# Gate accumulation pinned to its place in the vector queue, and a split moved behind two products

## The chip, the cores and the metric

The kernel runs on one core of one Trainium2 chip. The metric is device microseconds of one execution; the median of several runs counts. Within the core, TensorE (PE) multiplies, VectorE (DVE), ScalarE (ACT) and GpSimd (POOL) work element by element, and SyncE (SP) issues most of the loads. Each engine takes its instructions from its own queue, in order.

## What is computed

Two layers of a diffusion backbone, for 128 context tokens and 512 latent tokens (640 in all, width 1024). Layer 0 mixes tokens with attention and a state-space scan, layer 1 with pooling. Each layer ends with a dense SwiGLU feed-forward network (FFN). The change lies in the FFN and in the gates that scale its output:

```python
def modulation(cvec, w_mod, b_mod):
    m = jnp.expand_dims(jax.nn.silu(cvec) @ w_mod + b_mod, -2)
    return split_last(m, (D_MODEL,) * 6)          # shift, scale, gate of both sub-layers

def swiglu(h, w_gate, w_up, w_down):
    return (jax.nn.silu(h @ w_gate) * (h @ w_up)) @ w_down
...
fp = swiglu(modulate(xp, norm_pre_ffn[l], shf_p, scf_p), ffn_w_gate[l], ffn_w_up[l], ffn_w_down[l])
xp = xp + gf_p * rmsnorm(fp, norm_post_ffn[l])    # gf: gate, from the modulation
```

Everything is float32. A product is made of three matmuls over a high and a low part of each operand (high by high, high by low, low by high), so each weight and each activation is first split into two parts.

## The kernel before

**The FFN** (`_ffn`, line 538) has 22 tiles of 128 hidden columns, taken in 11 pairs. Each pair has two matrices, gate and up. The first pair is done by `plain` (line 644) in eight products. The other 20 matrices run in one loop (line 686, `n` from 2 to 21; even `n` is gate, odd is up), each by seven block products p1, p2, p5, p6, p7, p4, p3 of 12 matmuls over 320 columns (line 535). Between the products, five calls of `d()` (line 699) each do one piece of the down projection of the pair before (`down_add`, line 626: six matmuls of lines 98 to 100, then an add into `y` at line 632; for the first pair a ScalarE copy, line 630), and then one step of background work, `net.bg()` (line 149). The last pair's matrices (n=20, 21) have no down pieces, but call the background work.

**The path from a product to the next.** p1 fills PSUM bank A, and line 569 on ScalarE copies it out. p6 adds to the same bank, so it waits for line 569. Likewise line 579 copies p6's result before p7, and line 587 copies p7's before p4. p3 ends the matrix: line 596 (VectorE) adds, then line 598 (ScalarE, gate) or line 600 (VectorE, up). Line 574 (VectorE) adds p2's result, line 588 p7's. `out_split` (line 606) splits a finished ff tile into `ah` (ScalarE, line 609) and `al` (line 610, GpSimd or VectorE); the down pieces need both. The weights are split by `split` (lines 90 and 91: `ha`, `la` and so on; `hw`, `lw` are those of the down projection). GpSimd makes the sums of weight blocks (`adds`, lines 505 to 508). `A.fourth()` (line 432) splits the block `s4` of the activations into `a2h` and `a2l` (lines 441, 442).

**The gates.** `mod_gate_mac` (line 279) computes one half (512 columns) of one gate on VectorE as background work. It is a generator; each `yield` ends a step. For each of four `u` it loads 512 KB into `mraw` (line 289, SyncE; one buffer), and two steps later and again one step later makes a pair of multiply-adds into `macc` (line 295, 128x512). The first pair reads the bias `bb`. Then for both vectors `v` a ScalarE copy (line 303) and a VectorE subtract (line 304) split the sum, two matmuls (308, 309) add up the partitions, line 310 scales, and line 311 stores to `gd` in DRAM. Two steps lie between the split and the matmuls. That is 22 steps per half, 16 of them for the accumulation. Layer 0 queues four halves (88 steps), layer 1 two (44). They are queued by `env["gates"]()` at n=4 (line 690).

**What sets the order.** The kernel is written as one sequence. A planner fixes the order of each engine's queue when the program is built: it goes through the written instructions with its own estimate of times, and puts an instruction on its engine as soon as its inputs are ready by that estimate, earlier-written ones first where several are ready. So an instruction can stand in its queue ahead of others that were written before it. At run time the queues are fixed, and each instruction waits for what it needs.

Of the kernel before, what the change touches and what calls it, by code (L numbers as in the profile page):

```python
# [9 lines left out]
F32 = mybir.dt.float32  # L10
F32R = mybir.dt.float32r
BF16 = mybir.dt.bfloat16
AF = mybir.ActivationFunctionType
ALU = mybir.AluOpType
# [31 lines left out]
class Net:  # L46
# [144 lines left out]
    def mod_pairs(self, q, load, bufs):  # L191
# [13 lines left out]
                yield None  # L205
        yield out

    def mod_vec_tile(self):
        return self.md.tile([P, KC, 2], F32, tag="mv", name=self.name("mv"), bufs=6)

# [68 lines left out]
    def mod_gate_mac(self, dst, l, j, half, gain):  # L279
        nc = self.nc  # L280
        c0 = half * 512
        bb = self.bb
        gb = self.mrp.tile([P, 512], F32, tag="gb", name=self.name("gb"), bufs=1)
        nc.scalar.dma_start(bb[0:1], self.t["b_mod"][l, j * D + c0 : j * D + c0 + 512].unsqueeze(0))
        nc.scalar.dma_start(gb, self.t[gain][l, c0 : c0 + 512].partition_broadcast(P))
        acc = self.mrp.tile([P, 2, 512], F32, tag="macc", name=self.name("macc"), bufs=1)
        for u in range(4):
            x = self.mrp.tile([P, 1024], F32, tag="mraw", name=self.name("mraw"), bufs=1)
            nc.sync.dma_start(x, self.t["w_mod"][l, 2 * j + half, u])
            yield  # L290
            yield
            for k2 in range(2):
                kc = 2 * u + k2
                for v in range(2):
                    nc.vector.scalar_tensor_tensor(  # L295
                        acc[:, v], x[:, k2 * 512 : k2 * 512 + 512], self.silc[:, kc, v : v + 1],
                        acc[:, v] if kc else bb, op0=ALU.mult, op1=ALU.add,
                    )
                yield
        for v in range(2):  # L300
            h = self.mrp.tile([P, 512], F32R, tag="modh", name=self.name("modh"), bufs=1)
            lo = self.mrp.tile([P, 512], F32R, tag="modl", name=self.name("modl"), bufs=1)
            nc.scalar.activation(h, acc[:, v], AF.Copy)
            nc.vector.tensor_tensor(lo, acc[:, v], h.bitcast(F32), ALU.subtract)
            yield
            yield
            out = self.pt([P, 512])
            nc.tensor.matmul(out, self.oner, h, start=True, stop=False)
            nc.tensor.matmul(out, self.oner, lo, start=False, stop=True)
            nc.vector.tensor_tensor(acc[:, v], out, gb, ALU.mult)  # L310
            nc.scalar.dma_start(dst[v : v + 1, c0 : c0 + 512], acc[0:1, v])
            yield
# [225 lines left out]
def _ffn(net, l, A, fr, sp, tails, switch, finish):  # L538
    nc, t = net.nc, net.t
# [66 lines left out]
    def out_split(g, f, eng=None):  # L606
        ah = env["at"].tile([P, TOK], F32R, tag="ah", name=net.name("ah"))
        al = env["at"].tile([P, TOK], F32R, tag="al", name=net.name("al"))
        nc.scalar.activation(ah, g.s[:, f], AF.Copy)  # L609
        (eng or nc.gpsimd).tensor_tensor(al, g.s[:, f], ah.bitcast(F32), ALU.subtract)  # L610
        return ah, al

    def down_load(q, dh):
        return net.raw(t["w_down"][l, q, dh])
# [11 lines left out]
    def down_add(tt, dh, parts, first):  # L626
        out = down(tt, dh, parts)
        yd = env["y"][:, tt, dh * 512 : dh * 512 + 512]
        if first:
            nc.scalar.activation(yd, out, AF.Copy)  # L630
        else:
            nc.vector.tensor_tensor(yd, yd, out, ALU.add)  # L632
# [9 lines left out]
    s0 = sp.tile([P, 2, TOK], F32, tag="sg", name=net.name("sg"))  # L642

    def plain(m, f, half):
        out = net.pt([P, HB])
        wh, wl = (x.rearrange("p (k n) -> p k n", k=KC) for x in w0[m, f])
        net.mm3(out, [(wh[:, k], wl[:, k], bh, bl) for k, (bh, bl) in enumerate(A.plain(half))])
        d = s0[:, f, half * HB : half * HB + HB]
        if m is g0:
            nc.scalar.activation(d, out, AF.Silu)  # L650
        else:
            nc.vector.tensor_tensor(d, d, out, ALU.mult)
# [23 lines left out]
    at0 = [out_split(Out(s0), 0)]  # L676
# [2 lines left out]
    plain(g0, 1, 1)  # L679
    n1.c()  # L680
    plain(u0, 1, 1)
    at0.append(out_split(Out(s0), 1, nc.vector))
    prev = at0
    wdn = net.split(fr, "w", down_load(0, 0), None)
    last = {}
    for n, m in enumerate(seq, 2):
        p, up = divmod(n, 2)
        if n == 4:
            env["gates"]()
        w = Work(m, wg if up else None)  # L690
        if not up:
            wg = w
        nx = seq[n - 1] if n - 1 < len(seq) else None
        final = p == NPAIR - 1
        if final and not up:
            last[0, 0] = net.split(fr, "w", down_load(NPAIR - 2, 0), None)
        fill = [] if final else list(range(NT))

        def d():
            if fill:  # L700
                down_add(fill.pop(0), up, [(prev, wdn)], p == 1)
            net.bg()

        if nx:
            nx.load()
        w.p1()
        w.p2()
        m.b()
        if final and up:
            last[1, 0] = net.split(fr, "a", down_load(NPAIR - 1, 0), None)  # L710
        w.p5()
        w.p6()
        m.d()
        if nx:
            nx.a()
        d()
        if n == 2:
            A.fourth()
        d()
        w.p7()  # L720
        if nx:
            nx.adds()
        d()
        if nx:
            nx.c()
        if final and up:
            last[0, 1] = net.split(fr, "c", down_load(NPAIR - 2, 1), None)
        d()
        w.p4()
        if up:  # L730
            at = [out_split(wg, 0)]
        d()
        w.p3()
        if up:
            at.append(out_split(wg, 1, nc.vector if final else None))
        if up:
            if final:
                last[1, 1] = net.split(fr, "b", down_load(NPAIR - 1, 1), None)
                last["at"] = (prev, at)
            prev = at  # L740
        if nx and (n + 1) // 2 < NPAIR - 1:
            wdn = net.split(fr, "w", down_load((n + 1) // 2 - 1, (n + 1) % 2), None)
# [656 lines left out]
def trunk(ctx: ExitStack, tc: tile.TileContext, t: dict, o: dict):  # L1399
# [188 lines left out]
    def ffn(l, lag, ws, gates, finish):  # L1588
        es = ExitStack()
        a2 = es.enter_context(pool("a2", "left"))  # L1590
        sp = es.enter_context(pool("sg", "left", 3))
        tmp = ws.enter_context(pool("stmp", "right"))
        A.second(a2, tmp)
        rs, ms = ExitStack(), ExitStack()

        def switch(env):
            ws.close()
            env["y"] = y
            env["at"] = rs.enter_context(pool("at", "right", 4))
            env["mac"] = ms.enter_context(pool("mac", "right"))  # L1600
            env["gates"] = gates

        def fin(tail):
            es.close()
            ms.close()
            r = finish(tail, rs.enter_context(pool("gpr", "right")))
            rs.close()
            return r

        return _ffn(net, l, A, fr, sp, lag, switch, fin)  # L1610
# [218 lines left out]
```

## Time and profile before

| | us |
|---|---|
| median of 3 runs | 1431.85 |
| lowest, highest | 1430.41, 1436.32 |
| the profiled execution, its own time | 1430.04 |
| its span, first to last instruction | 1428.3 |

| engine | busy us | share of the span | instructions |
|---|---|---|---|
| TensorE matmul | 1359.2 | 95% | 7902 |
| TensorE weight load | 1164.9 | 82% | 7902 |
| VectorE | 987.5 | 69% | 1471 |
| ScalarE | 637.7 | 45% | 1140 |
| GpSimd | 413.0 | 29% | 341 |

Times in the rows are microseconds from the start of the span. The FFN loop runs from 501 to about 897 in layer 0 and from 1005 in layer 1. Weight loads overlap the matmuls of TensorE, so the two lines don't add up. In a row of the timeline, brackets show how long the engine had idled before it and what released it.

### The profile page before, as it was taken

Reading aid. Unit: us, or ns where it says so; the run is one execution under the profiler, and the core shown is the slowest. Engines: PE = TensorE matmul, PEld = TensorE weight load, DVE = VectorE, ACT = ScalarE, POOL = GpSimd, SP = SyncE. Lnnn points to the kernel's source line nnn. Section 1 sums busy time; section 2 is a strip of 40 time slices with the busy share of each in tenths; the row PEclk is TensorE's granted clock in tenths of the full one; section 3 lists DMA queues with packets and bytes.
Section 4 is the critical chain, followed back from the end, with each engine's and each line's share of the span. In section 5 each row is a group of like instructions: output and inputs, shape, how many; then the busy total and the mean of one; then the engine's idle time right before and its main releaser. Section 6 shows DMA issues by size and latency. Waiting matters only on the chain.

```text
span 1428.3 us, 20357 instructions
## 1 busy us (share of the span) xinstructions
PE 1359.2 (95%) x7902; PEld 1164.9 (82%) x7902; DVE 987.5 (69%) x1471; ACT 637.7 (45%) x1140; POOL 413.0 (29%) x341
## 2 busy tenths in 40 slices
PE   5999999999999889999999999898899999999997
PEld 2888765676668878998998999798889998999996
DVE  3765548867836876568778697787866686666657
ACT  3544634753424644343333444477443434334433
POOL 0100034253400344333333333002433334333320
PEclk9999989999999999999999999999999999999999
DMA  9344435700154233223233233521332232322213
GB/s 376 124 133 144 135 117 185 246 15 16 39 162 155 89 126 104 89 91 123 91 110 119 91 123 119 208 104 42 101 116 89 89 112 78 114 89 89 89 45 147
DMA packets 50277, 165.45 MB, mean 116 GB/s; under 512 B 5939, under 2 KB 9523, under 8 KB 50053
## 3 DMA queue, kind: packets, MB, share of 16 engines
q1 hardware_dynamic: 43488, 155.04, 32.3%
q10 hardware_dynamic: 6692, 9.11, 2.0%
q8 instruction: 62, 1.02, 0.3%
q14 instruction: 35, 0.28, 0.1%
HBM read 155.57 MB, written 8.56 MB: 115 GB/s over the span
## 4 chain that ended last, share of the span: by engine, by line
PE 70%; DVE 13%; DMA 7%; issue 4%; ACT 3%; POOL 1%; POOLq 0%; ACTq 0%; DVEq 0%; SPq 0%
PE ps L535 26%; PE ps L98 10%; PE ps L100 10%; PE ps L99 10%; DMA mraw<-in_w_mod 4%; DVE macc L295 4%; PE ps L183 2%; PE ps L1275 1%; PE ps L1374 1%; PE ps L1681 1%; PE ps L1083 1%; DMA band<-in_band 1%; DVE a2l L442 1%; PE ps L1257 1%; PE ps L1237 1%
## 5 line engine op out<-in xcount | busy, mean ns | idle before, releaser
L505 POOL TENSOR_TENSOR q<-raw,raw 128x512 f32<-128x512 f32 x40 | 57.3, 1433 | 356.7 <-DMA raw<-in_w_up 109.9
L100 PE MATMUL ps<-hw,al 128*128 128x512 f32 x380 | 151.2, 398 | 2.4 <-POOL al L610 1.8
L99 PE MATMUL ps<-lw,ah 128*128 128x512 f32 x380 | 151.3, 398 | 2.0 <-DVE lw L91 2.0
L98 PE MATMUL ps<-hw,ah 128*128 128x512 f32 x380 | 151.6, 399 | 0.6 <-ACT ah L609 0.6
L632 DVE TENSOR_TENSOR y<-y,ps 128x512 f32<-128x512 f32 x180 | 121.1, 684 | 37.4 <-PE ps L100 35.0
L535 PE MATMUL ps<-a2h,hc 128*128 128x320 f32 x320 | 99.6, 311 | 6.1 <-ACT sg L569 6.1
L535 PE MATMUL ps<-a2h,hb 128*128 128x320 f32 x320 | 99.9, 312 | 4.8 <-ACT sg L579 3.5
L295 DVE SCALAR_TENSOR_TENSOR macc<-mraw,silc,macc 128x512 f32<-128x512 f32 x84 | 80.6, 988 | 32.5 <-DMA mraw<-in_w_mod 32.4
L610 POOL TENSOR_TENSOR al<-sg,ah 128x640 fp32r<-128x640 f32 x40 | 75.5, 1887 | 94.9 <-ACT ah L609 86.2
L535 PE MATMUL ps<-a2h,lc 128*128 128x320 f32 x320 | 99.2, 310 | 0.0
L535 PE MATMUL ps<-a2l,hc 128*128 128x320 f32 x320 | 99.2, 310 | 0.0
L535 PE MATMUL ps<-a1h,la 128*128 128x320 f32 x320 | 99.0, 309 | 0.2 <-DVE la L91 0.2
L535 PE MATMUL ps<-a2h,lb 128*128 128x320 f32 x320 | 99.0, 309 | 0.0
L535 PE MATMUL ps<-a2l,hb 128*128 128x320 f32 x320 | 99.0, 309 | 0.0
L535 PE MATMUL ps<-a1h,ha 128*128 128x320 f32 x320 | 98.9, 309 | 0.0
L535 PE MATMUL ps<-a1l,ha 128*128 128x320 f32 x320 | 98.8, 309 | 0.0
L100 PEld LDWEIGHTS ps<-hw,al 128*128 128x128 f32 x380 | 71.8, 189 | 20.5 <-POOL al L610 2.7
L508 POOL TENSOR_TENSOR t<-raw,q 128x512 f32<-128x512 f32 x40 | 56.8, 1420 | 100.4 <-DVE ld L91 67.8
L99 PEld LDWEIGHTS ps<-lw,ah 128*128 128x128 f32 x380 | 72.3, 190 | 14.9 <-DVE lw L91 2.7
L98 PEld LDWEIGHTS ps<-hw,ah 128*128 128x128 f32 x380 | 72.4, 191 | 13.3 <-ACT ah L609 1.5
L90 ACT ACTIVATE hd<-t 128x512 fp32r<-128x512 f32 x40 | 25.3, 632 | 123.4 <-PE ps L535 115.7
L91 DVE TENSOR_TENSOR lc<-q,hc 128x1024 fp32r<-128x1024 f32 x40 | 50.3, 1257 | 35.6 <-ACT hc L90 35.5
(446 smaller groups left out, 3925.1 us busy)
## 6 DMA issues: line engine op xcount, KB each, us to landing
raw<-in_w_mod SPq DMA_DIRECT2D x56, 512.0 KB, 4.2
raw<-in_w_gate SPq DMA_DIRECT2D x44, 512.0 KB, 3.8
raw<-in_w_up SPq DMA_DIRECT2D x44, 512.0 KB, 4.1
raw<-in_w_down SPq DMA_DIRECT2D x44, 512.0 KB, 3.6
mraw<-in_w_mod SPq DMA_DIRECT2D x40, 512.0 KB, 4.6
xs<-xd SPq DMA_DIRECT2D x10, 512.0 KB, 5.9
x<-in_x_sample SPq DMA_DIRECT2D x8, 512.0 KB, 6.9
raw<-in_w_xbc SPq DMA_DIRECT2D x8, 512.0 KB, 6.2
```

The lines of the kernel that those rows point to most:

```text
L90: self.nc.scalar.activation(h, x, AF.Copy)
L91: (eng or self.nc.vector).tensor_tensor(l, x, h.bitcast(F32), ALU.subtract)
L98: mm(out, ah, bh, start=first and i == 0, stop=False)
L99: mm(out, ah, bl, start=False, stop=False)
L100: mm(out, al, bh, start=False, stop=last and i == n - 1)
L183: nc.tensor.matmul(out[32 * g : 32 * g + 32], self.silc[:, kc], x[:, k2 * 512 : k2 * 512 + 512], start=kc < 4, stop=kc >= 4,)
L295: nc.vector.scalar_tensor_tensor(acc[:, v], x[:, k2 * 512 : k2 * 512 + 512], self.silc[:, kc, v : v + 1], acc[:, v] if kc else bb, op0=ALU ...
L505: g.tensor_tensor(self.q[:, lo], self.rb[:, lo], self.ra[:, lo], ALU.subtract)
L508: g.tensor_tensor(self.t4, self.ra[:, hi], self.q[:, hi], ALU.subtract)
L535: mm(out, x[:, k], z[:, k], start=first and n == 0, stop=n == len(terms) - 1, skip_group_check=True)
L610: (eng or nc.gpsimd).tensor_tensor(al, g.s[:, f], ah.bitcast(F32), ALU.subtract)
L632: nc.vector.tensor_tensor(yd, yd, out, ALU.add)
```

## The change

The helper `pin` calls the planner's `keep_in_program_order`. It adds an edge from the instruction to the one written just before it on the same engine: the instruction can't be placed ahead of that one in the queue. It is an order only, with no wait at run time. It is put on the multiply-adds of line 295, and on lines 303 and 304. The loads of `mraw` (line 289) and the rest of the gate work are not pinned.

The second part moves one call. The split of the second ff tile of the first pair was written ahead of the split of the down weights and the loop. It now stands in the loop's first round (n=2), after p1 and p2 and ahead of `m.b()`.

```diff
+    def pin(self, ins):
+        return self.tc.keep_in_program_order(ins)
...
-                    nc.vector.scalar_tensor_tensor(
+                    self.pin(nc.vector.scalar_tensor_tensor(
                         acc[:, v], x[:, k2 * 512 : k2 * 512 + 512], self.silc[:, kc, v : v + 1],
                         acc[:, v] if kc else bb, op0=ALU.mult, op1=ALU.add,
-                    )
+                    ))
...
-            nc.scalar.activation(h, acc[:, v], AF.Copy)
-            nc.vector.tensor_tensor(lo, acc[:, v], h.bitcast(F32), ALU.subtract)
+            self.pin(nc.scalar.activation(h, acc[:, v], AF.Copy))
+            self.pin(nc.vector.tensor_tensor(lo, acc[:, v], h.bitcast(F32), ALU.subtract))
...
     plain(u0, 1, 1)
-    at0.append(out_split(Out(s0), 1, nc.vector))
     prev = at0
...
         w.p1()
         w.p2()
+        if n == 2:
+            at0.append(out_split(Out(s0), 1, nc.vector))
         m.b()
```

## Rows read from the trace of the kernel before

**Rows 1.** The page: busy time by engine (section 1), chain by line (section 4)

```profile
PE 1359.2 (95%) x7902; PEld 1164.9 (82%) x7902; DVE 987.5 (69%) x1471; ACT 637.7 (45%) x1140; POOL 413.0 (29%) x341
...
PE ps L535 26%; PE ps L98 10%; PE ps L100 10%; PE ps L99 10%; DMA mraw<-in_w_mod 4%; DVE macc L295 4%; PE ps L183 2%; PE ps L1275 1%; PE ps L1374 1%; PE ps L1681 1%; PE ps L1083 1%; DMA band<-in_band 1%; DVE a2l L442 1%; PE ps L1257 1%; PE ps L1237 1%
```

**Rows 2.** Timeline, TensorE, first matmul of a matrix: start, us, engine, line, operation

```profile
501.48 0.31 PE L535 MATMUL ps<-a1h,ha 128*128 128x320 f32 x1
...
526.29 0.31 PE L535 MATMUL ps<-a1h,ha 128*128 128x320 f32 x1
...
551.41 0.31 PE L535 MATMUL ps<-a1h,ha 128*128 128x320 f32 x1
...
570.70 0.31 PE L535 MATMUL ps<-a1h,ha 128*128 128x320 f32 x1
...
668.10 0.31 PE L535 MATMUL ps<-a1h,ha 128*128 128x320 f32 x1
...
690.12 0.31 PE L535 MATMUL ps<-a1h,ha 128*128 128x320 f32 x1
...
748.93 0.31 PE L535 MATMUL ps<-a1h,ha 128*128 128x320 f32 x1
...
789.07 0.31 PE L535 MATMUL ps<-a1h,ha 128*128 128x320 f32 x1
...
1004.64 0.31 PE L535 MATMUL ps<-a1h,ha 128*128 128x320 f32 x1
...
1029.57 0.31 PE L535 MATMUL ps<-a1h,ha 128*128 128x320 f32 x1
...
1053.63 0.31 PE L535 MATMUL ps<-a1h,ha 128*128 128x320 f32 x1
...
1170.32 0.31 PE L535 MATMUL ps<-a1h,ha 128*128 128x320 f32 x1
...
1192.06 0.31 PE L535 MATMUL ps<-a1h,ha 128*128 128x320 f32 x1
```

**Rows 3.** Waits of TensorE, 500 to 900: total us, times, longest

```profile
PE ps L535 <- ACT sg L569: 5.6, 3, 2.7
```

**Rows 4.** Timeline of VectorE, 506 to 586; brackets: idle before, and releaser

```profile
506.28 1.78 DVE L295 SCALAR_TENSOR_TENSOR macc<-mraw,silc,bb 128x512 f32<-128x512 f32 x1
...
508.38 2.16 DVE L442 TENSOR_TENSOR a2l<-y,a2h 128x1280 fp32r<-128x1280 f32 x1
...
510.46 1.92 DVE L610 TENSOR_TENSOR al<-sg,ah 128x640 fp32r<-128x640 f32 x1
...
512.31 1.21 DVE L91 TENSOR_TENSOR lw<-raw,hw 128x1024 fp32r<-128x1024 f32 x1
...
530.12 1.41 DVE L295 SCALAR_TENSOR_TENSOR macc<-mraw,silc,macc 128x512 f32<-128x512 f32 x2 [3.19 <-DMA mraw<-in_w_mod]
...
585.29 0.69 DVE L632 TENSOR_TENSOR y<-y,ps 128x512 f32<-128x512 f32 x1 [0.71 <-PE ps L100]
```

**Rows 5.** Timeline of ScalarE, 508 to 546

```profile
508.49 0.74 ACT L609 ACTIVATE ah<-sg 128x640 fp32r<-128x640 f32 x1 [1.33 <-DVE sg L652]
...
533.10 0.74 ACT L598 ACTIVATE sg<-sg 128x640 f32<-128x640 f32 x1 [5.70 <-DVE sg L596]
...
545.39 0.63 ACT L303 ACTIVATE modh<-macc 128x512 fp32r<-128x512 f32 x1 [4.18 <-DVE macc L295]
```

**Rows 6.** DMA issues (page, section 6): count, size, us to landing

```profile
mraw<-in_w_mod SPq DMA_DIRECT2D x40, 512.0 KB, 4.6
```

**Rows 7.** Windows: length, busy PE, PEld, DVE, ACT, POOL, clock, DMA, GB/s

```profile
520.00:540.00 20.00, 17.48 (x95) 15.73 (x94) 12.77 (x16) 8.62 (x13) 6.03 (x4) 0.91 0.39 135
560.00:600.00 40.00, 40.00 (x237) 37.04 (x236) 25.12 (x31) 14.85 (x21) 14.44 (x10) 1.00 0.27 89
```

**Rows 8.** Waits of TensorE, 1000 to 1428

```profile
PE ps L100 <- DVE al L610: 0.6, 1, 0.6
```

**Rows 9.** Instructions on tile macc: ns min/median/max, first and last start

```profile
L295 DVE SCALAR_TENSOR_TENSOR macc<-mraw,silc,macc x84: 737/744/2067, 515.6 to 1180.4; 128x512 f32<-128x512 f32 x84
```

## The prediction

> **What bounds the kernel now.** I read the page first: TensorE is busy 95% of the span, and the chain that ended last is mostly its matmuls. But the same chain holds the loads of `mraw` (4%) and the vector steps of line 295 (4%), about 110 us in which the end of the kernel hung on the gate accumulation [rows 1]. So TensorE is the bound, and I looked for the places where it is held up.
>
> For that I took the start of each matrix, which is its first matmul with `ha`. From n=4 to n=5 is 570.70 - 551.41 = 19.29 us, and in that stretch nothing stalls. Every period over 19.29 is a loss [rows 2]:
> - layer 0: n=2 lasts 24.81 (5.52 lost), n=3 25.12 (5.83), n=10 22.02 (2.73), n=14 and 15 together 40.14 (1.56)
> - layer 1: n=2 lasts 24.93 (5.64), n=3 24.06 (4.77), n=10 21.74 (2.45)
>
> That is 28.5 us in all. In layer 0 the largest waits of TensorE are for L569, the ScalarE copy of p1's output, which must be out before p6 may add to that bank [rows 3].
>
> Why is L569 late? In n=3 VectorE stands 3.19 us at a line-295 step whose `mraw` has not landed (at 530.12 [rows 4]). Line 596 queues behind it, so ScalarE's line 598 idles 5.70 us for 596, and L569 queues behind 598 (at 533.10 [rows 5]). Later in n=3 ScalarE stands 4.18 us at line 303 for the accumulation, with L587 and thus p4 behind it (at 545.39 [rows 5]). The code starts the gates at n=4, at 551.41, yet the first line-295 step runs at 506.28 [rows 4]: the planner pulled the accumulation 45 us forward into slots where, by its own estimate, the data had landed. A load takes 4.6 us to land [rows 6].
>
> The clock adds to it: in 520 to 540 the mean granted clock is 0.91, so TensorE ran at 1.2 instead of 2.4 GHz for some 0.09 x 2 x 20 = 3.6 us, in a stretch where it had just idled for L569; in 560 to 600, without a stall, it is 1.00 [rows 7]. This cost is inside the periods above, and should go with the stalls.
>
> **Part 1: the pins.** They add no instruction and no wait at run time. They only fix the order: each line-295 step now stands behind the vector instruction written before it, which is the `y` add (L632) of the same d() step, and lines 303 and 304 likewise on their queues. The `mraw` loads are not pinned, but each needs the one buffer that the pinned steps free, so they slow down with them. A half takes 16 of its 22 background steps for the accumulation, so its pairs of line 295 spread over some three matrices (about 60 us); the first half now takes 39, from 506.28 to line 303 at 545.39 [rows 4, 5].
> - n=3 of both layers: nothing of the gates is left there, since they begin at n=4. I take the whole loss, 5.8 and 4.8.
> - n=10, 14 and 15 of layer 0 and n=10 of layer 1: these fall in the pulled-forward bursts of later halves. I take 2.7 + 1.55 + 2.45. If something else stalls there, 0.
> - n=2, layer 0: the accumulation's first step (1.78 us [rows 4]) leaves; the rest belongs to part 2.
> - n=2, layer 1: the late half of the stall is ScalarE behind the accumulation; what stays is a wait of 0.6 us for `al` of line 610 [rows 8] and the small ones beside it.
>
> What do the pinned steps cost where they now stand? There are 48 pairs in 27 matrices (88 background steps in layer 0, 44 in layer 1, five to a matrix). VectorE is busy 25.12 of 40 us in the clean stretch, so it has 7.2 us free in 19.29 [rows 7]. A step takes 0.744 us at the median and 2.067 at most [rows 9], a pair 1.5 to 4.1; 1.8 pairs per matrix take 2.7 to 7.4. So VectorE has room at the median and none at the worst. What is queued behind a pair? The worst place is the fifth d(): there lines 91 (`lw`), 596, 598 and 569 follow, and p6 waits for L569. Between the end of p3 and p6 lie p1, p2 and p5. Two d() steps back to back are 0.71 + 0.69 = 1.40 apart (at 585.29 [rows 4]), so a product is (19.29 - 5 x 1.40) / 7 = 1.76 and the cover is 5.3 us. From it go `lw` (1.21 [rows 4]), the pair (1.5) and the chain 596, 598, 569 (an estimate of 1.6, from 0.74 for 598 [rows 5] and about half of it for each of the two shorter ones). About 1.0 us is left over. With a 4.1 us pair, 1.6 us would be missing. Counting the steps, 9 pairs stand at a fifth d(), so they cost 0 to 14 us. Then the loads: a new `mraw` is issued when the pair before is done and needed three d() steps later. The shortest such way is first to fourth d(): three d() and p7 are 6.0 us, less about 1.5 for the pair, so 4.5 against 4.6 to land. That occurs 3 times; the other ways are longer. I take 3 us for all of this together, near the median end, as that is where most rows are, and keep 0 and 14.
>
> The shared port of VectorE and GpSimd speaks against the change. Rows first: the same step takes 0.737 to 2.067 us [rows 9]. The Trainium skill ("SBUF — State Buffer", Who interferes with whom) says that a vector instruction with two SBUF inputs and a GpSimd instruction that reads SBUF exclude each other, the loser blocking until the other is done; a line-295 step is of that kind, and the spread of its durations agrees. By that rule the pairs behind the first to third d(), where GpSimd makes the next matrix's adds, would be the slow ones; what that makes of the time is the rival "half comes back" below, 1421.
>
> At the end of layer 0 the accumulation now ends only in n=20 (its 82nd background step, five to a matrix from n=4), but its last matmul stands in n=21 as before and the store of `gd[1]` follows that. I take nothing; 2 us either way is possible.
>
> **Part 2: the split of the second ff tile.** Two instructions move behind p1 and p2: ScalarE's copy `ah` and VectorE's `al`. In layer 0 `ah` idled 1.33 us for line 652, with L569 queued behind it (at 508.49 [rows 5]). After the move L569 no longer waits for that and for the 0.74 of `ah` itself, so p6 can start about 2 us sooner. But `al` (1.92 us) is still needed by the second half of the first d(). VectorE must do line 652, `a2l` (2.16), `lw` (1.21), line 574 and `al` (1.92) from about 506.3 on [rows 4], some 6.2 us in sequence, so `al` is done near 512.4. In the kernel before, that matmul came at about 514.5: `lw` was out at 513.5, and four more of the six matmuls of a 1.40 us d() followed. So layer 0's n=2 gains 2.2 of its 5.5 (bounds 0 and 5.5: none if `al` is the last in any order, all if `lw` and `al` are taken ahead of `a2l`). In layer 1 `al` was already the last thing and now comes after line 574, 0.5 us later; the ScalarE stall behind it goes. I take 3.6 of 5.6 (bounds 0 and 5).
>
> **Sum.** Layer 0: 2.2 + 5.8 + 2.7 + 1.55 = 12.25. Layer 1: 3.6 + 4.8 + 2.45 = 10.85. Together 23.1, less 3 for new waits: 20 us. The profiled execution took 1430.04 us (span 1428.3), 1.8 below the median 1431.85; it would come to 1410, and the median to 1412.
>
> **Rivals.**
> - Half comes back. The pairs meet GpSimd's adds and the 9 at a fifth d() cost about 1.0 us each on top of the 3: 23.1 - 12 = 11 gained, 1421. For it: the slow rows up to 2.067. Against it: the median of 0.744.
> - The first matrices stay slow. With the accumulation away, n=2 and n=3 wait for something else, such as the weight splits or loads that queue in the same stretch; then only the later 6.7 us and a little more are gained, less the 3: about 1426. Against it: n=4, with all the same splits, runs without a stall.
> - Slower: VectorE becomes the bound. If pairs in their written place take 4.1 us or more, the 1.8 per matrix fill its 7.2 us of idle time, and every product's copy queues. It is slower than before once each of the 27 matrices loses over 23.1 / 27 = 0.86 us; at 1.2 us it gives 1441. Only the largest row speaks for it.
> - The pins do nothing, and the pairs still run before n=4. Then only part 2's 2.2 us is left: 1430. The order is fixed when the program is built, so I count this inside the 0.07 of the case above.
>
> **How the numbers follow.** Forecast 1412, chance 0.70, own range 1406 to 1418. Half comes back 0.18 (1417 to 1427). First matrices stay slow 0.07. Slower 0.05. The range 1405 to 1424 takes in the first and most of the second. A measurement of this kernel can tell about 0.5%, 7 us, from no change: under 1424.7 lie the first case and most of the second, 0.85; within 0.5% 0.10; slower 0.05.
>
> **What would show it.** Right: no line-295 step before n=4 (so none in the first 50 us of either layer's FFN after the up and gate products of pair 0); periods of n=3 and n=10 near 19.3; L569 of n=2 ahead of the second `ah`; granted clock 1.00 in n=2 and n=3; VectorE's waits for `mraw` shorter than the 3.19 us above, or covered. Wrong: periods of 20 and more spread over n=4 to 20, with TensorE waiting for L569 or `al`; or a stall in n=3 that has another releaser than a line-295 step.

## The result and the profile after

The median went from 1431.13 us (4 runs) to 1414.2 (4 runs, 1413.28 to 1417.99), a ratio of 0.9871, 95% interval 0.985 to 0.9893. The profiled execution took 1413.28 us, its span 1411.5 against 1428.3. Lines of the changed kernel stand 3 further down as far as the loop: the products are L538, p1's copy is L572, the multiply-adds L298, `modh` and `modl` L306 and L307, `ah` and `al` L612 and L613.

The page of the changed kernel, busy time by engine and chain by line:

```profile
PE 1355.1 (96%) x7902; PEld 1165.9 (83%) x7902; DVE 1003.7 (71%) x1471; ACT 637.3 (45%) x1140; POOL 419.5 (30%) x341
...
PE ps L538 30%; PE ps L98 11%; PE ps L100 11%; PE ps L99 11%; PE ps L183 2%; PE ps L1378 1%; PE ps L1279 1%; DMA mraw<-in_w_mod 1%; PE ps L1685 1%; DVE a2l L445 1%; PE ps L1087 1%; DVE macc L298 1%; PE ps L1261 1%; PE ps L1241 1%; DVE wl L83 1%
```

`mraw` and `macc` had 4% each of the chain [rows 1]; they have 1% each. The counts are the same: nothing was taken away. VectorE is even busier, by 16.2 us.

Timeline of TensorE after, first matmul of a matrix (layer 0: n=2, 3, 4, then 20; layer 1: n=2, 3, 4, then 20):

```profile
501.64 0.31 PE L538 MATMUL ps<-a1h,ha 128*128 128x320 f32 x1
...
526.38 0.31 PE L538 MATMUL ps<-a1h,ha 128*128 128x320 f32 x1
...
545.68 0.31 PE L538 MATMUL ps<-a1h,ha 128*128 128x320 f32 x1
...
857.96 0.31 PE L538 MATMUL ps<-a1h,ha 128*128 128x320 f32 x1
...
998.58 0.31 PE L538 MATMUL ps<-a1h,ha 128*128 128x320 f32 x1
...
1019.89 0.31 PE L538 MATMUL ps<-a1h,ha 128*128 128x320 f32 x1
...
1039.18 0.31 PE L538 MATMUL ps<-a1h,ha 128*128 128x320 f32 x1
...
1349.86 0.31 PE L538 MATMUL ps<-a1h,ha 128*128 128x320 f32 x1
```

The same of the kernel before, n=20 of both layers (its other starts are in [rows 2]):

```profile
867.18 0.31 PE L535 MATMUL ps<-a1h,ha 128*128 128x320 f32 x1
...
1366.63 0.31 PE L535 MATMUL ps<-a1h,ha 128*128 128x320 f32 x1
```

Differences of such starts, in us (those of n=10 to 17 are read in the same view):

| stretch | before | after | gain | forecast |
|---|---|---|---|---|
| layer 0, n=2 | 24.81 | 24.74 | 0.07 | 2.2 |
| layer 0, n=3 | 25.12 | 19.30 | 5.82 | 5.8 |
| layer 0, n=10 | 22.02 | 19.66 | 2.36 | 2.7 |
| layer 0, n=14 and 15 | 40.14 | 38.59 | 1.55 | 1.55 |
| layer 0, n=16 | 19.76 | 20.19 | -0.43 | in the 3 for new waits |
| layer 1, n=2 | 24.93 | 21.31 | 3.62 | 3.6 |
| layer 1, n=3 | 24.06 | 19.29 | 4.77 | 4.8 |
| layer 1, n=10 | 21.74 | 19.41 | 2.33 | 2.45 |
| n=20 of layer 0 to n=2 of layer 1 | 137.46 | 140.62 | -3.16 | 0, 2 either way |

With the start of the first loop 0.16 later that makes 16.8 of the span's 16.8. Two rows miss: n=2 of layer 0, and the stretch between the layers. Both spans are of one execution each; the kernel before alone ran from 1429.26 to 1436.32 us, so the rows tell where these two executions differ, and the medians (16.9 us apart) carry the result.

Waits of VectorE after, 495 to 900: total, times, longest:

```profile
DVE macc L298 <- DMA mraw<-in_w_mod: 2.5, 2, 1.3
```

In the kernel before this was 19.6 us in 8 waits over the same stretch. On tile `macc`, ns min/median/max, first and last start:

```profile
L298 DVE SCALAR_TENSOR_TENSOR macc<-mraw,silc,macc x84: 736/786/2055, 562.4 to 1190.0; 128x512 f32<-128x512 f32 x84
L298 DVE SCALAR_TENSOR_TENSOR macc<-mraw,silc,bb x12: 740/1296/1800, 559.5 to 1136.8; 128x512 f32<-128x512 f32 x12
```

The first multiply-add runs at 559.5, inside n=4 (from 545.68), where it is written; before it ran at 506.28 [rows 4]. Windows after:

```profile
500.00:520.00 20.00, 16.36 (x91) 15.24 (x90) 14.46 (x14) 9.97 (x15) 11.65 (x6) 0.91 0.44 146
520.00:540.00 20.00, 20.00 (x119) 18.52 (x118) 7.28 (x9) 10.33 (x16) 7.56 (x6) 1.00 0.25 79
```

From 520 to 540 TensorE has no gap and the full clock (17.48 us and 0.91 before [rows 7]). From 500 to 520 it still stalls, and the clock there is 0.91 and not the 1.00 that the prediction gave as a sign of being right. The waits of TensorE from 495 to 560 come down to one row:

```profile
PE ps L538 <- ACT sg L572: 3.6, 1, 3.6
```

VectorE and ScalarE behind that wait (timeline after; brackets: idle before, and releaser):

```profile
506.62 2.57 DVE L445 TENSOR_TENSOR a2l<-y,a2h 128x1280 fp32r<-128x1280 f32 x1
509.11 0.47 DVE L655 TENSOR_TENSOR sg<-sg,ps 128x320 f32<-128x320 f32 x1
```

```profile
509.62 0.74 ACT L612 ACTIVATE ah<-sg 128x640 fp32r<-128x640 f32 x1 [2.11 <-DVE sg L655]
510.26 0.42 ACT L572 ACTIVATE sg<-ps 128x320 f32<-128x320 f32 x1
```

The multiply-add has left 506.28, and `a2l`, 2.57 us, has moved up into its slot, ahead of L655 (`plain`'s multiply, L652 before; there `a2l` came behind it, at 508.38 [rows 4]). The second `ah` waits for L655, and p1's copy L572 still stands behind `ah`: the call was moved behind p1 in the text, and the planner put it ahead again.

### The profile page after: what moved, and what is told of

Its sections match the earlier page's. It is cut to its first block, busy times and chain, and to the rows that moved or that the text cites. A ratio compares the mean times of both kernels' runs of the same rounds, so it can differ in the third digit from the quotient of the medians.

```text
span 1411.5 us, 20377 instructions
## 1 busy us (share of the span) xinstructions
PE 1355.1 (96%) x7902; PEld 1165.9 (83%) x7902; DVE 1003.7 (71%) x1471; ACT 637.3 (45%) x1140; POOL 419.5 (30%) x341
## 4 chain that ended last, share of the span: by engine, by line
PE 78%; DVE 9%; ACT 4%; DMA 3%; issue 3%; POOL 1%; POOLq 0%; ACTq 0%; DVEq 0%; SPq 0%
PE ps L538 30%; PE ps L98 11%; PE ps L100 11%; PE ps L99 11%; PE ps L183 2%; PE ps L1378 1%; PE ps L1279 1%; DMA mraw<-in_w_mod 1%; PE ps L1685 1%; DVE a2l L445 1%; PE ps L1087 1%; DVE macc L298 1%; PE ps L1261 1%; PE ps L1241 1%; DVE wl L83 1%
## 5 line engine op out<-in xcount | busy, mean ns | idle before, releaser
L613 POOL TENSOR_TENSOR al<-sg,ah 128x640 fp32r<-128x640 f32 x40 | 75.8, 1894 | 96.0 <-ACT ah L612 90.4
L538 PE MATMUL ps<-a2h,hc 128*128 128x320 f32 x320 | 99.5, 311 | 3.6 <-ACT sg L572 3.6
L538 PE MATMUL ps<-a2h,hb 128*128 128x320 f32 x320 | 99.0, 309 | 1.7 <-ACT sg L582 1.7
L538 PE MATMUL ps<-a2h,lc 128*128 128x320 f32 x320 | 99.4, 311 | 0.0
L538 PE MATMUL ps<-a2l,hc 128*128 128x320 f32 x320 | 99.3, 310 | 0.0
L538 PE MATMUL ps<-a1h,la 128*128 128x320 f32 x320 | 99.0, 309 | 0.2 <-DVE la L91 0.2
L538 PE MATMUL ps<-a1h,ha 128*128 128x320 f32 x320 | 98.9, 309 | 0.0
L538 PE MATMUL ps<-a1l,ha 128*128 128x320 f32 x320 | 98.8, 309 | 0.0
L538 PE MATMUL ps<-a2l,hb 128*128 128x320 f32 x320 | 98.8, 309 | 0.0
L538 PE MATMUL ps<-a2h,lb 128*128 128x320 f32 x320 | 98.8, 309 | 0.0
L298 DVE SCALAR_TENSOR_TENSOR macc<-mraw,silc,macc 128x512 f32<-128x512 f32 x84 | 93.6, 1155 | 3.4 <-DMA mraw<-in_w_mod 3.4
```

Of the source, the lines that this page charges most:

```text
L298: self.pin(nc.vector.scalar_tensor_tensor(acc[:, v], x[:, k2 * 512 : k2 * 512 + 512], self.silc[:, kc, v : v + 1], acc[:, v] if kc else bb ...
L538: mm(out, x[:, k], z[:, k], start=first and n == 0, stop=n == len(terms) - 1, skip_group_check=True)
```

## The experiments

Two questions were open. First, how did the early multiply-adds hold TensorE up: because VectorE stood waiting for `mraw` (the prediction's reason), or because their own work stood ahead of steps that TensorE needed? Second, what do the move and the written place of the steps do by themselves? Where nothing else is said, an edit is to the changed kernel, and ratios are to the kernel before, timed again beside each group of runs (its median lay between 1432.85 and 1434.91).

**Pins alone.**

```diff
+    at0.append(out_split(Out(s0), 1, nc.vector))
...
-        if n == 2:
-            at0.append(out_split(Out(s0), 1, nc.vector))
```

> The changed kernel without its second part: the split of the second ff tile is back in its old written place, the pins stay. Theory (the move did nothing, because the planner still put the second ah ahead of the copy of p1's output): the same time as the changed kernel, 1414 within 4 us, and n=2 of layer 0 again at 24.7 us with TensorE waiting some 3.6 us for the copy. Rival (the move carried the 2.2 us forecast for it, and something else took them away again): 2 to 3 us slower, n=2 over 26 us.

1414.81 us, ratio 0.9868 (0.9845 to 0.9891). n=2 of layer 0 takes 24.69 us with 3.58 of wait for L572; n=2 of layer 1 takes 21.31. The order of the instructions on all five engines is that of the changed kernel, so the move has no part in the gain.

**Move alone.** The kernel before with the call moved, no pin.

> The kernel before with the move of the second ff tile's split alone, no pin. Theory (the move is without effect, because the planner still places the split ahead of p1's copy): layer 0's n=2 lasts 24.8 us and n=3 25.1 us as before, and the ratio to the kernel before lies between 0.998 and 1.002. Rival (the move brings its forecast 2.2 us by itself, and in the changed kernel something else took them back): n=2 lasts 22 to 23 us, ratio 0.998 or less, n=3 as before or shorter.

1433.14 us, ratio 0.9991 (0.9977 to 1.0004). n=2 and n=3 of layer 0 take 25.47 and 24.55, together 50.02 against 49.93. Only one neighbouring pair on VectorE, `al` and `lw`, has changed places.

**Loads away, work left.** The kernel before, with one load per half, reused for all four `u`; three of four weight loads of the gates are left out.

```diff
-            x = self.mrp.tile([P, 1024], F32, tag="mraw", name=self.name("mraw"), bufs=1)
-            nc.sync.dma_start(x, self.t["w_mod"][l, 2 * j + half, u])
+            if u == 0:
+                x = self.mrp.tile([P, 1024], F32, tag="mraw", name=self.name("mraw"), bufs=1)
+                nc.sync.dma_start(x, self.t["w_mod"][l, 2 * j + half, u])
```

> The kernel before, without pins, where each half of a gate loads its weights once and uses them for all four u; it leaves out three of four gate weight loads, so the gates are computed from the wrong weights, with every multiply-add still done. It tells the two costs of the early accumulation apart. Load theory (TensorE was held up because VectorE stood at multiply-adds whose mraw had not landed): with no load to wait for, layer 0's n=3 falls from 25.1 to 21 us or less, n=2 and n=3 lose together less than 5 of the 11.35 us. Displaced-work theory (VectorE does 0.74 us multiply-adds ahead of the steps that TensorE needs, and the planner, seeing no load, puts even more of them there): n=2 and n=3 lose together 9 us or more. The pins cure both, so the time of the changed kernel can't tell them apart.

1431.74 us, ratio 0.9977 (0.9957 to 0.9997). n=2 and n=3 of layer 0 take 24.50 and 23.97 and lose 9.89 us together, against 11.35 before, as the displaced-work theory has it. VectorE's wait for `mraw` in 500 to 560 is gone (10.1 us in the kernel before), but TensorE's wait for p1's copy in that stretch (lines here are 1 further down than before: L570 is the copy) is

```profile
PE ps L536 <- ACT sg L570: 5.6, 2, 2.9
```

where the kernel before has 5.2. VectorE and then ScalarE of this kernel (timeline; L296 is the multiply-add):

```profile
524.25 6.81 DVE L296 SCALAR_TENSOR_TENSOR macc<-mraw,silc,macc 128x512 f32<-128x512 f32 x6
...
532.53 1.98 DVE L91 TENSOR_TENSOR lw<-raw,hw 128x1024 fp32r<-128x1024 f32 x1 [0.26 <-ACT hw L90]
534.43 0.47 DVE L597 TENSOR_TENSOR sg<-sg,ps 128x320 f32<-128x320 f32 x1
```

```profile
530.43 0.63 ACT L304 ACTIVATE modh<-macc 128x512 fp32r<-128x512 f32 x1 [4.77 <-DVE macc L296]
...
534.94 0.74 ACT L599 ACTIVATE sg<-sg 128x640 f32<-128x640 f32 x1 [1.49 <-DVE sg L597]
535.58 0.42 ACT L570 ACTIVATE sg<-ps 128x320 f32<-128x320 f32 x1
```

No step waits for a load, yet six multiply-adds in a row fill 6.81 us, ScalarE stands 4.77 us at `modh` for their sum, and `lw`, L597, L599 and L570 come after them. So early multiply-adds hold TensorE up without any wait for a load.

The edit doesn't tell how the kernel before divides between the two causes, because the planner's order has changed with it. Multiply-adds in n=2 of layer 0 (window; length, VectorE on their line, clock, DMA share, GB/s), before and in this run:

```profile
501.48:526.29 24.81, 8.38 (x8) 1.00 0.39 129
```

```profile
503.24:527.74 24.50, 11.46 (x13) 1.00 0.32 110
```

It has 13 there where the kernel before has 8, so work may have taken the place of waits. In layer 1 the two matrices lose 7.12 us against 10.41. What the waits for loads cost in the kernel before stays open; the 1.5 us of layer 0 and the 3.3 of layer 1 are what came back with this order.

**Multiply-adds pinned, `modh` and `modl` not.**

```diff
-            self.pin(nc.scalar.activation(h, acc[:, v], AF.Copy))
-            self.pin(nc.vector.tensor_tensor(lo, acc[:, v], h.bitcast(F32), ALU.subtract))
+            nc.scalar.activation(h, acc[:, v], AF.Copy)
+            nc.vector.tensor_tensor(lo, acc[:, v], h.bitcast(F32), ALU.subtract)
```

> The changed kernel without the pins on modh and modl: only the multiply-adds are pinned. Theory (the multiply-adds carry the gain, and modh and modl can't run before the last of them): 1412 to 1418, ratio 0.985 to 0.989, n=3 of both layers 19.3. Rival (modh and modl, placed early by the planner, hold ScalarE and VectorE back where the accumulation is late): stalls with modh or modl as releaser or with p4's copy behind them, 1419 or more.

1409.09 us (1408.93 to 1415.31), ratio 0.9847 (0.9818 to 0.9876); n=3 takes 19.30 and 19.29. The time is below what was expected, but its interval overlaps that of the changed kernel, and the loops take 355.96 and 352.20 us against 356.32 and 351.28: no difference is shown. Beside the pins on the multiply-adds, those on lines 306 and 307 show no gain.

**`modh` and `modl` pinned, multiply-adds not.**

```diff
-                    self.pin(nc.vector.scalar_tensor_tensor(
+                    nc.vector.scalar_tensor_tensor(
```

> The changed kernel without the pins on the multiply-adds: only modh and modl are pinned, and the split is moved. Theory (the early multiply-adds are the damage): 1428 to 1434, layer 0's n=2 and n=3 lose together 9 us or more. Rival (the damage is ScalarE standing for the sum at the early modh, with p4's copy behind it): n=3 falls to 22 or less in layer 0, 1425 or less.

1428.49 us, ratio 0.9964 (0.9946 to 0.9981). n=2 and n=3 of layer 0 take 25.53 and 22.87 and lose 9.82 us. A few us are gained, most of them in layer 1 (its loop 358.39 against 361.99): n=3 there falls from 24.06 to 20.37, as TensorE's wait for p7's copy, which stood behind the early `modh`, is gone. The pins on the multiply-adds bring this without those; most of the gain needs them.

**The second split really behind p1's copy.**

```diff
-    def out_split(g, f, eng=None):
+    def out_split(g, f, eng=None, pin=lambda ins: ins):
...
-        nc.scalar.activation(ah, g.s[:, f], AF.Copy)
+        pin(nc.scalar.activation(ah, g.s[:, f], AF.Copy))
...
         w.p1()
-        w.p2()
         if n == 2:
-            at0.append(out_split(Out(s0), 1, nc.vector))
+            at0.append(out_split(Out(s0), 1, nc.vector, net.pin))
+        w.p2()
```

> The changed kernel with the second split written right behind p1 and its ScalarE copy ah pinned there, so that it stands behind the copy of p1's output on ScalarE; nothing else differs. Theory (that copy was late because it stood behind ah, which waits for VectorE's line 652 multiply): the 3.6 us wait at p6 in n=2 of layer 0 falls under 0.6, the following down piece waits 1 to 2 us for lw and al instead, n=2 takes 22 to 23 us instead of 24.7, and the kernel gains about 2 us. Rival (VectorE's a2l step sets n=2, and the order on ScalarE does not matter): n=2 stays at 24 to 25 us.

1412.5 us (1408.86 to 1417.8), ratio 0.986 (0.9828 to 0.9891). n=2 of layer 0 takes 23.35: the wait for the copy falls from 3.64 to 0.72, and 1.35 for `lw` and 0.65 for `al` come in its place. The gain is 1.39 us, a little under the forecast's 2.2. The time can't be told from the changed kernel's.

**That, and `A.fourth`'s split in its written place.**

```diff
-        self.split(h[:, self.S4], l[:, self.S4], self.s4, self.net.nc.vector)
+        nc = self.net.nc
+        x, hh, ll = self.s4, h[:, self.S4], l[:, self.S4]
+        self.net.pin(nc.scalar.activation(hh, x, AF.Copy))
+        self.net.pin(nc.vector.tensor_tensor(ll, x, hh.bitcast(F32), ALU.subtract))
```

> As the kernel with ah pinned, and the split of the fourth activation block (a2h, a2l) is pinned in its written place behind the first down piece too, so its 2.57 us of VectorE time no longer stand ahead of the multiply, lw and al. Theory (both orders hold n=2 up): n=2 of layer 0 falls to 20 to 21 us, n=2 of layer 1 from 21.3 to 20 to 21, and the kernel is 4 to 6 us faster than the changed one, near 1409. Rival (the a2l step is covered anyway): no gain over pinning ah alone.

1409.65 us, ratio 0.9838 (0.9816 to 0.986). n=2 takes 20.77 in layer 0 and 19.29 in layer 1.

**`A.fourth`'s split in its written place alone** (the diff just above; the second split as in the changed kernel).

> The changed kernel with A.fourth's split (a2h, a2l) pinned in its written place and the second ff tile's split left as it is. With both pinned, layer 0's n=2 fell from 24.74 to 20.77 us; with the second split alone pinned, to 23.35. Theory (the 2.57 us a2l ahead of the weight splits is the larger cost, independent of the other): n=2 of layer 0 22 us or less, layer 1's n=2 19.3 to 20. Rival (p1's copy still stands behind the second ah, so p6 waits as before): n=2 of layer 0 24 us or more, with the wait of p6 for p1's copy over 2.5 us.

1406.85 us (1405.98 and 1407.72), ratio 0.9821 (0.9788 to 0.9854). n=2 takes 20.92 and 19.29: nearly all that both pins brought. VectorE and ScalarE (L658 is the multiply that was L655, L575 p1's copy, L615 `ah`):

```profile
506.57 0.47 DVE L658 TENSOR_TENSOR sg<-sg,ps 128x320 f32<-128x320 f32 x1
506.97 1.92 DVE L91 TENSOR_TENSOR lw<-raw,hw 128x1024 fp32r<-128x1024 f32 x1
...
514.58 1.49 DVE L440 TENSOR_TENSOR a2l<-y,a2h 128x1280 fp32r<-128x1280 f32 x1 [0.47 <-ACT a2h L439]
```

```profile
507.08 0.74 ACT L615 ACTIVATE ah<-sg 128x640 fp32r<-128x640 f32 x1 [0.78 <-DVE sg L658]
507.72 0.42 ACT L575 ACTIVATE sg<-ps 128x320 f32<-128x320 f32 x1
```

`ah` still stands ahead of p1's copy, and that is harmless: with `a2l` out of the way the multiply starts 2.5 us sooner (506.57 against 509.11), and the copy with it (507.72 against 510.26). TensorE's wait for it is 1.2 us. Most of the stall of n=2 was `a2l`, 3.82 of the 5.45 us over 19.29; the split that the change moved had less.

**Gates queued one matrix earlier.**

```diff
-        if n == 4:
+        if n == 3:
             env["gates"]()
```

> The changed kernel with the gates queued at n=3 instead of n=4, so every background step stands one matrix earlier. Theory (the new 1.4 and 0.5 us waits of TensorE in n=20 of layer 0 come from the last half standing so late that its two matmuls and the first products of n=21 no longer fill the gap between p6 and p7): both waits go, n=20 and 21 together return to about 29 us from 30, and the kernel gains 1 to 2 us, unless pairs in n=3 cost as much there. Rival (those waits are the price of pinned pairs in any last matrix): they move to another matrix and nothing is gained.

1411.48 us, ratio 0.9853 (0.983 to 0.9876). n=3 stays at 19.29, so a pinned accumulation may start there. The two waits of n=20 (for the copies of p6 and p7, 1.41 and 0.53 us) go, but others come in n=20, n=21 and right behind them: 0.74 for `modl`, 1.11 for `lc`, 0.77 for `al`, 0.32 for `lb`. From n=20 to layer 1 it takes 140.69 us, as in the changed kernel.

**The last three edits together.**

> The changed kernel with the second split pinned behind p1's copy, A.fourth's split pinned in its written place, and the gates queued at n=3 instead of n=4. Theory (the gains add up where they lie in different matrices): layer 0's n=2 20.8 and layer 1's n=2 19.3 as with the pinned splits alone, n=3 of both 19.3; the waits of n=20 for the copies of p6 and p7 go, but up to 3 us of others come there, as with the earlier gates alone; 1407 to 1411, ratio 0.982 to 0.985. Rival (a first load and first pairs one matrix earlier press the late splits): n=3 over 20.5, 1412 or more.

1409.08 us (1406.69 to 1410.8), ratio 0.9829 (0.9807 to 0.9851). The sum holds as expected, but `A.fourth`'s split in its written place gives as much by itself. All runs of both lie below the lowest of the changed kernel, 1413.28, while the intervals of the ratios still touch.

**Double dose.** After each multiply-add a second pinned one, with a column of zeros: it adds nothing to the sum.

```diff
+                    self.pin(nc.vector.scalar_tensor_tensor(
+                        acc[:, v], x[:, k2 * 512 : k2 * 512 + 512], self.silc[:, kc, 31:32],
+                        acc[:, v], op0=ALU.mult, op1=ALU.add,
+                    ))
```

> The changed kernel with a second pinned multiply-add behind each of the 96, which adds zero: 96 x 0.74 = 71 us more of VectorE's time in written place. It measures the reserve. Theory (VectorE has 7.2 us free in a clean matrix, the pairs took 2.7 of them and take 5.4 now; only at the 9 fifth d() steps is the reserve of 1.0 us too small by 0.5): 2 to 10 us over the changed kernel, 1416 to 1424, periods of most matrices 19.3 to 20.3. Rival (VectorE is already near the bound and each pair more queues a copy that TensorE waits for): each matrix with pairs loses 0.75 us or more, 20 us or more in all, 1434 or more.

1449.16 us, ratio 1.0101 (1.0077 to 1.0126): 35 us over the changed kernel (33 by the two ratios), and the theory's 2 to 10 fell. Its count was wrong: 5.4 us of pairs in a matrix is the mean over all 27, at the median duration; the matrices that hold pairs hold more. The time VectorE spends on `macc` in n=4 to n=7 of layer 0 (window; length, VectorE, ScalarE, clock, DMA share, GB/s), in the changed kernel and with the double dose:

```profile
545.68:564.97 19.29, 4.30 (x4) 0.00 (x0) 1.00 0.25 83
564.97:584.26 19.29, 4.97 (x4) 0.00 (x0) 1.00 0.44 136
584.26:603.56 19.30, 4.82 (x5) 0.00 (x0) 1.00 0.35 110
603.56:623.32 19.76, 6.28 (x7) 1.25 (x2) 1.00 0.35 108
```

```profile
546.59:565.88 19.29, 4.87 (x6) 0.00 (x0) 1.00 0.27 83
565.88:585.17 19.29, 8.81 (x11) 0.00 (x0) 1.00 0.35 110
585.17:608.26 23.09, 9.42 (x10) 0.00 (x0) 1.00 0.33 95
608.26:634.35 26.09, 11.01 (x11) 1.25 (x2) 0.87 0.30 99
```

**Half dose.** The added step only behind the second multiply-add of a pair.

```diff
+                    if v:
+                        self.pin(nc.vector.scalar_tensor_tensor(
...
```

> The changed kernel with one added pinned multiply-add of zero per pair instead of two: 48 x 0.74 = 36 us more of VectorE's time, half the dose of the double one, which cost 35 us. Threshold theory (n=4 to n=6 leave VectorE 2.6 to 3.1 us free, and the half dose adds some 2.2 us to a matrix; with the double one the matrix with 8.81 us of multiply-adds lost nothing and those with 9.42 and 11.01 lost 3.8 and 6.8): 0 to 8 us over the changed kernel, 1414 to 1422. Rival (each added step queues a copy that TensorE waits for, in proportion): half of 35, 1430 to 1434.

1419.34 us (1417.96 to 1420.36), ratio 0.9911 (0.9885 to 0.9937): 5 us more than the changed kernel for half the dose, 35 for the whole (the intervals of the ratios of this run and of the changed kernel overlap by a little). So the cost doesn't grow in proportion to the dose. The same four matrices:

```profile
541.78:561.08 19.30, 4.98 (x5) 0.00 (x0) 1.00 0.25 82
561.08:580.37 19.29, 7.32 (x8) 0.00 (x0) 1.00 0.33 110
580.37:599.98 19.61, 6.95 (x6) 0.00 (x0) 1.00 0.33 108
599.98:620.62 20.64, 6.54 (x9) 1.25 (x2) 1.00 0.40 128
```

Matrices with 4.3 to 5.0 us lose nothing; 7.32, 6.95 and 6.54 lose 0, 0.3 and 0.9 (n=7 takes 19.76 undisturbed). With the double dose 8.81 loses nothing yet, but the next two, with 9.42 and 11.01, lose 3.8 and 6.3. In these four the losses begin near the 7.2 us that the prediction found free, in a stretch without multiply-adds. It is no sharp line: what else stands in the queue counts too. n=11 with the double dose holds 9.69 us and loses nothing, and n=10 of the changed kernel holds more than 7.2 and is 0.4 us over 19.29:

```profile
662.37:682.03 19.66, 8.44 (x6) 0.00 (x0) 1.00 0.37 108
```

## Why the prediction was right, and where it was not

**The pins: right, for a reason that was only part of it.** The terms for n=3, 10, 14 and 15 were taken whole from the periods, and they came out within 0.4 us each. The cause that the prediction gave, VectorE standing for `mraw`, is in the rows (3.19 us in n=3 [rows 4]), but the damage doesn't need it: without loads 9.89 of 11.35 us stayed lost in layer 0. Early work in the queue held TensorE up with or without waits for loads; their shares in the kernel before are open. For this change both causes give the same forecast, since the pins take the work away from there; for one that only made the loads earlier they would not.

**Part 2 failed, as a step.** The prediction posed "the change does nothing" only for the pins, not for the move. The planner, which places an instruction as soon as it holds it ready, put `ah` ahead of p1's copy either way; the move alone has the ratio 0.9991. So the 2.2 us of layer 0 did not come (0.07), and two of the prediction's signs failed with them: L572 still stands behind the second `ah`, and the clock in n=2 isn't 1.00. Nor would the step have been the right one: forced into place the split gives 1.39, and `a2l` in its written place gives 3.82 (24.74 to 20.92) without it. The bound named in the prediction (all, if `lw` and `al` are taken ahead of `a2l`) pointed at it; the likeliest value assumed that `a2l` stays where it was, while in fact it moved up into the slot that the multiply-add left. The rival "the first matrices stay slow" is this mechanism; it is true in part, in n=2 of both layers.

**Layer 1's n=2: the number right by luck.** 3.62 us came, 3.6 were forecast, but the pins alone give the same 21.31 and the split's move has no share in it. The remaining 2.02 us are `a2l` again (19.29 when it is pinned).

**New waits: 3 us forecast, 3.6 measured, elsewhere and partly by luck.** The nine fifth d() steps, where the prediction looked, show no wait for L572; n=16 lost 0.43 us, with a wait of 0.17 for GpSimd's `al`. n=20 and 21 of layer 0 lost 1.1 us: TensorE waits 1.41 and 0.53 us for the copies of p6 and p7 there. Some 2 us more went between the layers, where the order on TensorE is the same. That part goes with the clock. From n=20 to layer 1, before and then after; columns as in [rows 7]:

```profile
867.18:1004.64 137.46, 127.18 (x772) 116.70 (x771) 105.63 (x179) 85.90 (x191) 23.95 (x15) 0.98 0.34 122
```

```profile
857.96:998.58 140.62, 129.57 (x772) 118.53 (x771) 107.30 (x184) 86.65 (x192) 24.70 (x16) 0.95 0.34 119
```

TensorE is busy 2.39 us longer with as many matmuls, and idle 0.77 us more. The lower clock isn't tied to the pins on the multiply-adds. The run with one load per half (no pin, TensorE's order there as before) has 0.95 too, and takes 141.24 us; the run with the multiply-adds alone pinned has 0.98, and takes 139.85. The prediction had no term for these 2 us, and without them the new waits are about 1.5 us, half of the forecast. Each kernel was traced once, so a difference between executions isn't ruled out.

**The rival "half comes back" and the shared port.** The pairs did become slower. The group of line 298, 84 steps (busy us, mean ns), before and after:

```profile
L295 DVE SCALAR_TENSOR_TENSOR macc<-mraw,silc,macc 128x512 f32<-128x512 f32 x84 | 80.6, 988 | 32.5 <-DMA mraw<-in_w_mod 32.4
```

```profile
L298 DVE SCALAR_TENSOR_TENSOR macc<-mraw,silc,macc 128x512 f32<-128x512 f32 x84 | 93.6, 1155 | 3.4 <-DMA mraw<-in_w_mod 3.4
```

That is 13 us more of VectorE's time. Two neighbouring pairs of n=6, and GpSimd's first add beside the second of them:

```profile
594.27 1.41 DVE L298 SCALAR_TENSOR_TENSOR macc<-mraw,silc,macc 128x512 f32<-128x512 f32 x2
...
596.20 2.46 DVE L298 SCALAR_TENSOR_TENSOR macc<-mraw,silc,macc 128x512 f32<-128x512 f32 x2
```

```profile
596.47 1.63 POOL L508 TENSOR_TENSOR q<-raw,raw 128x512 f32<-128x512 f32 x1 [5.18 <-DVE y L635]
```

The rule of the Trainium skill ("SBUF — State Buffer", Who interferes with whom), that the two engines lock each other out of a shared port, agrees with these rows. But it cost TensorE next to nothing: n=4 to n=9 keep their 19.29 and 19.76 us, with 4.3 to 6.3 us of this work in n=4 to n=7, below the 7.2 that VectorE has free. Priced at the mean of 988 instead of the median of 744, the prediction's 1.8 pairs would have been 3.6 us instead of 2.7; it didn't matter here, but it helped to make the expectation of the double dose wrong.

**The rival "slower"** has the mechanism: it came true at the double dose, 1449.16 us. At the single dose n=4 to n=6 were still 2 to 3 us of VectorE's time below the 7.2.

## What to carry to other kernels

When a planner orders the queues, read an instruction's place from the trace, not from the text: background work can stand in front of urgent work, and moving a call in the text may change nothing, while an order edge on the right instruction does. When one early step is taken out of a queue, ask which other one moves up into its slot; here that was worth as much as a whole part of the change. For an engine's reserve count its work per stretch by mean durations in the densest stretch, and test it: here half the dose on top cost 5 us and a whole one 35.

## What was not expected of the hardware

After the change the granted clock is 0.67, a mean of its two levels of 1.2 and 2.4 GHz, in a stretch in which TensorE was busy all 5.00 us, and the 10 us ahead of it were as busy, at 1.00 and 0.99:

```profile
937.96:942.96 5.00, 5.00 (x22) 4.61 (x23) 3.41 (x8) 4.36 (x13) 0.00 (x0) 0.67 0.34 105
```

It fell near the end of 44 matmuls of 128 columns in a row. The kernel before does the same 44 from 940.87 in 4.97 us. They stand here after the change, then in the runs with one load per half and with the multiply-adds alone pinned:

```profile
933.31 5.25 PE L1378 MATMUL ps<-band,hn 128*128 128x128 f32 x44
```

```profile
946.46 6.02 PE L1375 MATMUL ps<-band,hn 128*128 128x128 f32 x44
```

```profile
929.74 4.97 PE L1378 MATMUL ps<-band,hn 128*128 128x128 f32 x44
```

TensorE did the same work ahead of them each time. At 4.97 us the clock stays at 1.00; at 6.02 it is 0.81. Of the fourteen traces, the fall at or right behind these matmuls is in seven. What decides it is open.
